# Where the modulation chunks and the next group's weights stand inside the down-projections of a SwiGLU

## The chip, the cores and the metric

The kernel runs on one core of a Trainium2 chip. The metric is the device time of one execution in microseconds (us). Before the change it was 2321.56 us, the median of three runs (2318.89, 2321.56 and 2325.57 us).

The engines are called PE (matrix products; PEld is its weight load), DVE (VectorE), ACT (ScalarE), POOL (GpSimd) and SP (SyncE, which here only issues DMA transfers).

## The reference

One inference step of a two-layer backbone, on 128 context rows and 512 latent rows of width 1024 (640 tokens in all). Each layer runs a SwiGLU, a mixer (layer 0: convolution and spatial gating; layer 1: windowed attention), and a second SwiGLU. Each of them is wrapped in a norm with a shift, a scale and a gate that come from the modulation vector:

```python
def modulation(cond, w_mod, b_mod):
    m = jax.nn.silu(cond) @ w_mod + b_mod
    return m.reshape(cond.shape[0], N_MOD, D_MODEL)       # 9 rows of 1024 per layer

def pre(x, m, g, slot):
    return rms_norm(x, g) * (1 + m[:, 3 * slot + 1][:, None, :]) + m[:, 3 * slot][:, None, :]

def residual(x, y, m, g, slot, weight):
    return x + weight * m[:, 3 * slot + 2][:, None, :] * rms_norm(y, g)

def swiglu(h, wg, wu, wd):                                # wg, wu: 1024 x 2816, wd: 2816 x 1024
    return (jax.nn.silu(h @ wg) * (h @ wu)) @ wd
```

All is float32. The modulation of both layers is read from `w_mod`, 2 x 1024 x 9216 numbers; the kernel reads it in 128-column chunks, of which 128 are worked in the background of the four SwiGLUs.

## The kernel before, in words

**Precision.** A float32 product is made of three products of halves: each weight chunk is loaded as a tile `raw` (128x1024 float32, 512 KB), ACT copies it into a rounded high half, DVE subtracts that from it for the low half (both tiles named `w`), and PE multiplies high by high, high by low and low by high.

**One SwiGLU.** `ffn` is called four times, layer by layer. The 2816 hidden columns are 22 tiles of 128, taken in parts: (0,5), (5,10), (10,16), (16,22) in the first SwiGLU, (0,4), (4,10), (10,16), (16,22) in the other three. A part computes its hidden tiles (gate, up, silu and product), and then `down` multiplies them with their rows of `wd`: ten steps (two halves of the output columns by five token tiles), each a run of PE products into one PSUM bank, an ACT copy `tmp<-ps` and a GpSimd transfer that adds it to `ys` in memory. The fourth part ends elsewhere (`last_products`).

**Groups.** The first tiles of a SwiGLU (ten in the first, four in the others) are computed the plain way. From tile `since` on `group` computes a tile by seven products p1 to p7 of sums, each of 12 matmuls with 320 columns. Their weights come from one array `ws` in three loads: G (512 KB, `load_gate`, into `raw`), the sums S (`load_sums`, into `rawx`, with an adding GpSimd transfer behind the load) and U (`load_up`, for two tiles at once, into `raw`). From them come these steps, named as in the code; a 0 is the ACT copy and a 1 the DVE subtraction:

- g0, g1: the halves of G (for p2, p1)
- s2: two DVE additions that turn G's buffer into weight sums; t0, t1: the halves of these (for p3, p6)
- s0, s1: the halves of S (for p7, p5)
- u0, u1: the halves of U (for p4)

A product is moved out of PSUM by e1 to e7: e1, e3, e5, e6 on ACT, e2, e4, e7 on DVE. p6 is accumulated in the bank of p1 and p5 in the same bank again, so p6 can start only behind e1 and p5 only behind e6. Inside a group the first tile's products come in the order p1, p2, p6, p7, p5. `go` runs a product, then the evacuation of the product before, then one entry of a list of fills, which prepare the next tile.

**The transition.** The weights of a group's first tile are prepared inside `down` of the part before: the list `between` has one entry for each of its ten steps, and the list `mods` says how many modulation chunks follow each step. In the text a step is called by its place: down step 0 to down step 9. The second tile's weights (written g0', g1' and so on) are prepared by the fills of the first tile's products, the third tile's are written g0'' and so on.

**Chunks.** `mod_chunk` takes one modulation chunk: a load of 512 KB from `wmodT` into `raw` by SP (line 536), then two DVE passes (`scr<-raw,cbc`, one for each of the two conditions), each with a short read of the accumulator. `background(n)` takes the next n chunks; `background_ahead` only issues the load of the next one. In a transition the chunks are here called m1, m2 and so on, in their order. Chunks are queued as 54, 33, 33 and 8 for the four SwiGLUs; the last one's list is used up within its first `down` and the group after it. Nine transitions into a group carry chunks: one behind a part of five tiles (first SwiGLU), five behind parts of six tiles (one in the first, two in the second, two in the third SwiGLU) and three behind parts of four tiles (second, third and fourth).

**What sets the order.** PE, DVE, ACT and POOL run in program order; nothing overtakes. SP issues its transfers in program order as well, and a transfer that waits for its buffer holds back all that stand behind it. The tile `raw` has three buffers in turn, so a load waits for the last reader of the third load before it. `rawx` has two. The loads of `wd`, of G, of U and of the chunks all share `raw`.

Of the kernel before, what the change touches and what calls it, by code (L numbers as in the profile page):

```python
# [89 lines left out]
class Builder:  # L90
# [548 lines left out]
    def ffn(self, l, i, h, lead, nxt, fetches, started=None):  # L639
# [9 lines left out]
        def weights(j):  # L649
            if j not in ws:  # L650
                ws[j] = [self.take(*self.ffn_weight(l, i, j, w)) for w in ("wg", "wu")]
            return ws[j]

        def unit(j, g, inserts=None):
            if j not in gs:
                gs[j] = self.pair()
            self.glu(*self.proj2(weights(j), h, g, inserts), gs[j], g)
# [24 lines left out]
        def load_sums(j):  # L682

            w = a["ws"][l, i, j]
            r = self.rawx()
            nc.sync.dma_start(out=r, in_=w[:, 512:1536])
            nc.gpsimd.dma_start(out=r.rearrange("p (a b) -> p a b", a=2),  # L687
                                in_=w[:, 1536:2048].unsqueeze(1).to_broadcast([P, 2, 512]), accum_op=ALU.add)
            raws["s", j] = r

        def load_gate(j):
            r = raws["g", j] = self.raw(D)
            nc.sync.dma_start(out=r, in_=a["ws"][l, i, j, :, 0:1024])

        def load_up(j):
            n = min(2, ends[j] - j)
            r = raws["u", j] = self.raw(n * 512)
            nc.sync.dma_start(out=r.rearrange("p (j m) -> p j m", j=n),
                              in_=a["ws"][l, i, j:j + n, :, 1024:1536].rearrange("j p m -> p j m"))
# [20 lines left out]
        def prep(j):  # L720


            def s2():
                r = raws["t", j] = raws["g", j]
                V.tensor_tensor(out=r[:, 512:1024], in0=raws["s", j][:, 512:1024], in1=r[:, 512:1024], op=ALU.add)
                V.tensor_tensor(out=r[:, 0:512], in0=r[:, 512:1024], in1=r[:, 0:512], op=ALU.add)

            g = halves("g", j, (2, j), (1, j))
            s = halves("s", j, (7, j), (5, j))
            t = halves("t", j, (3, j), (6, j))  # L730
            u = halves("u", j, (4, j), (4, j + 1)) if j in pairs else [lambda: None] * 2
            return dict(g0=g[0], g1=g[1], s2=s2, t0=t[0], t1=t[1], s0=s[0], s1=s[1], u0=u[0], u1=u[1])
# [68 lines left out]
        def run(fs):  # L801
            for f in fs:
                f()

        def wpieces(half, j0, j1):

            res = []

            def piece(j):
                m = min(2, j1 - j)  # L810
                res.extend(self.wload(a["wd"][l, i, j:j + m, :, half * 512:half * 512 + 512].rearrange("j p m -> p j m"), m, 512))

            return [lambda j=j: piece(j) for j in range(j0, j1, 2)], res
# [3 lines left out]
        def sums_between(every=1):  # L817
            return {k: lambda: run([tops.pop(0) for _ in range(1) if tops]) for k in range(0, KC, every)}
# [4 lines left out]
        def settle():  # L823

            for f, j in late[:]:
                if f is not p7 or (p5, j) in done:
                    late.remove((f, j))
                    evacs[f](j)
                    done.add((f, j))

        def go(f, j, *then):
            f(j)
            settle()
            late.append((f, j))
            run(then)

        def fills(n):

            if n >= NJ:
                return [[] for _ in range(7)]  # L840
            w = prep(n)
            return [[], [w["g0"]], [w["g1"]], [lambda: load_up(n), w["s2"]] if n in pairs else [w["s2"]], [w["t0"]],
                    [w["t1"], lambda: load_gate(n + 1) if n + 1 < ends[n] else None],
                    [w["s0"], w["s1"], lambda: load_sums(n + 2) if n + 2 < NJ else None]]

        def steps(j0, j1):

            r = [(p1, j0), (p2, j0), (p6, j0), (p7, j0), (p5, j0)]
            for j in range(j0 + 1, j1):
                r += [(p1, j), (p3, j - 1), (p6, j), (p4, j - 1), (p7, j), (p5, j), (p2, j)]  # L850
            return r

        def group(j0, j1, wd):


            fs = []
            ahead, mod = [self.background_ahead], [lambda: self.background(1)]
            for j in range(j0, j1):
                w = prep(j)
                f = fills(j + 1) if j + 1 < j1 else [[], [], wd[0:1], [], wd[1:2], [], wd[2:3]]  # L860
                u = [w["u0"], w["u1"]] if j in pairs else []
                if j == j0:
                    f = [u + ahead + f[1], f[2] + f[3], mod + f[4], f[5], ahead + f[6]]
                else:
                    f[0] = u + f[0]
                    if j + 1 < j1:
                        f[1] = f[1] + mod
                    if j + 2 < j1:
                        f[5] = f[5] + ahead
                fs += f  # L870
            for (p, j), f in zip(steps(j0, j1), fs):
                go(p, j, *f)
            go(p3, j1 - 1, *wd[3:4])
            go(p4, j1 - 1, *wd[4:])
            settle()
# [3 lines left out]
        def down(j0, j1, pi, wd):  # L879

            gp = [gs.pop(j) for j in range(j0, j1)]
            loads, wd2 = wpieces(1, j0, j1)
            if j1 < since:
                between = [loads, [], [], [], [], [], [lambda: weights(j1)], [], [], []]
                mods = [0, 2, 2, 1, 1, 1, 0, 1, 1, 1]
            else:
                n = prep(j1)
                between = [loads, [], [], [lambda: load_gate(j1)], [],
                           [n["g0"], n["g1"]], [n["s2"], n["t0"]], [n["t1"], lambda: load_gate(j1 + 1)],
                           [lambda: load_up(j1), n["s0"]], [n["s1"], lambda: load_sums(j1 + 2)]]  # L890
                mods = [0, 2, 2, 1, 1, 0, 0, 0, 0, 0]
            for half in range(2):
                for t in range(NT):
                    ps = self.ps()
                    self.proj_tok(ps, gp, (wd, wd2)[half], t)
                    o = self.tmp(512)
                    copy(o, ps)
                    nc.gpsimd.dma_start(out=ys[t, half], in_=o, **(dict(accum_op=ALU.add) if pi else {}))  # L898
                    run(between.pop(0))
                    self.background(mods.pop(0))  # L900

        for pi, (j0, j1) in enumerate(bounds[:-1]):
            loads, wd = wpieces(0, j0, j1)
            if j0 >= since:
                group(j0, j1, loads)
            elif not started:
                load_sums(since)
                load_sums(since + 1)
                unit(1, GB, sums_between())
                weights(3)  # L910
                unit(2, GB, sums_between())
                todo = sums_between()
                todo[2] = lambda then=todo[2]: (then(), run(loads))
                unit(3, GA, todo)
                run(tops)
                unit(3, GB)
            else:
                if j0 == 0:
                    unit(1, GB)
                    self.setup_cbc()  # L920
                    unit(2, GA)
                    weights(3)
                    self.background(2)
                    unit(2, GB)
                    self.background(2)
                else:
                    load_sums(since)
                    load_sums(since + 1)
                for j in range(max(j0, 3), j1):
                    weights(j)  # L930
                    if j + 1 < j1:
                        weights(j + 1)
                    else:
                        run(loads)
                    for n, g in enumerate(GROUPS):
                        unit(j, g, sums_between(2) if j0 else None)
                        self.background(1 if j0 else 2)
                if j0:
                    run(tops)
            down(j0, j1, pi, wd)  # L940
        j0, j1 = bounds[-1]
        rows = self.gate_rows(l, slot, True)
        wd = []
        group(j0, j1, [lambda j=j: wd.append(self.wload(a["wd"][l, i, j], 2, 512)) for j in range(j0, j1)])
        gp = [gs.pop(j) for j in range(j0, j1)]
        self.drain()
# [1014 lines left out]
```

## Time and profile before

| | us |
|---|---|
| median of three runs | 2321.56 |
| the profiled execution's own time | 2317.79 |
| its span in the trace | 2316.0 |
| PE busy | 2251.5 (97% of the span) |
| DVE busy | 1656.7 (72%) |
| ACT busy | 1048.5 (45%) |
| POOL busy | 282.2 (12%) |

The profiled execution took 1.8 us more than its span, and 3.8 us less than the median. A row of the trace's timeline reads: start, duration, engine, line, operation, output <- input, shape, count, and in brackets the idle time ahead of it with the instruction that ended it. Most rows carry line 71, the helper through which the engines' instructions are recorded, so rows are told apart by their tiles and shapes: `ps<-w,act` with 512 columns is the down-projection, `ps<-act,w` and `ps<-sum,w` with 320 columns are products of a group, `w<-raw,w` and `w<-rawx,w` on DVE are the steps whose names end in 1, and `scr<-raw,cbc` is a pass over a chunk.

### The profile page before, as it was taken

The numbers are of one execution on the slowest core, as the hardware profiler recorded it, in microseconds if no ns is written. First come the engines' busy times: TensorE is split into PE (matmuls) and PEld (weight loads), VectorE is DVE, ScalarE is ACT, GpSimd is POOL, SyncE is SP. The second block draws the span as 40 slices with busy tenths as digits, with TensorE's granted clock in tenths as the row PEclk, the third lists the DMA queues.
The fourth block names the chain that finished last, engine by engine and source line by source line (L and its number), as shares of the span: only waits on it lengthen the run. The fifth ranks groups of instructions, "written<-read, shape, count | busy, mean of one in ns | idle before, by whom it ended". The sixth has DMA issues, their size and how long they took to land.

```text
span 2316.0 us, 35260 instructions
## 1 busy us (share of the span) xinstructions
PE 2251.5 (97%) x13692; PEld 2039.6 (88%) x13692; DVE 1656.7 (72%) x2758; ACT 1048.5 (45%) x1845; POOL 282.2 (12%) x377
## 2 busy tenths in 40 slices
PE   9999999999999999999999999999989999999998
PEld 8989898989889898989798989898966798989896
DVE  5688777767867786868677777676788578636366
ACT  5223343453165443434554434345568564435352
POOL 1000111021002111110011011102121021111100
PEclk9999999999999999999999999999989999999999
DMA  8564868632224578785536687864000345666644
GB/s 306 169 231 153 220 180 213 187 139 89 76 101 124 183 196 200 192 199 162 217 111 209 181 213 179 212 189 154 36 21 10 128 120 192 171 135 156 140 125 173
DMA packets 137671, 370.07 MB, mean 160 GB/s; under 512 B 14464, under 2 KB 16384, under 8 KB 136736
## 3 DMA queue, kind: packets, MB, share of 16 engines
q1 hardware_dynamic: 103952, 299.93, 38.0%
q0 software_dynamic: 33552, 67.90, 16.8%
q8 instruction: 107, 1.75, 0.3%
q14 instruction: 60, 0.49, 0.1%
HBM read 322.90 MB, written 42.25 MB: 158 GB/s over the span
## 4 chain that ended last, share of the span: by engine, by line
PE 69%; DVE 14%; DMA 7%; issue 4%; ACT 4%; POOL 1%; SPq 1%; DVEq 0%; ACTq 0%; POOLq 0%
PE ps L71 69%; DVE tmp L71 4%; DVE w L71 2%; DVE scr L71 2%; DMA raw<-wmodT 2%; DMA ggrow<-grow 2%; ACT w L71 1%; DVE Y L71 1%; DMA Y<-ys 1%; DVE act L71 1%; POOL nwq L71 1%; ACT tmp L71 1%; DMA rawx<-ws 1%; ACT act L71 1%; DVE raw L71 1%
## 5 line engine op out<-in xcount | busy, mean ns | idle before, releaser
L71 PE MATMUL ps<-act,w 128*128 128x320 f32 (+6 forms) x6024 | 914.5, 319 | 18.5 <-DVE w L71 10.1
L71 PEld LDWEIGHTS ps<-act,w 128*128 128x128 f32 (+1 forms) x6024 | 847.6, 185 | 49.3 <-issue 18.1
L71 PE MATMUL ps<-w,act 128*128 128x512 f32 (+1 forms) x3480 | 793.0, 387 | 11.0 <-ACT act L71 7.8
L71 PEld LDWEIGHTS ps<-w,act 128*128 128x128 f32 x3480 | 632.1, 191 | 149.5 <-ACT act L71 9.7
L71 DVE TENSOR_TENSOR w<-raw,w 128x1024 fp32r<-128x1024 f32 (+1 forms) x340 | 410.7, 1221 | 191.2 <-ACT w L71 183.9
L71 PE MATMUL ps<-sum,w 128*128 128x320 f32 x3168 | 481.5, 310 | 6.9 <-ACT tmp L71 6.7
L71 PEld LDWEIGHTS ps<-sum,w 128*128 128x128 f32 x3168 | 469.1, 188 | 10.9 <-ACT tmp L71 10.9
L71 ACT ACTIVATE w<-raw 128x1024 fp32r<-128x1024 f32 (+1 forms) x340 | 350.7, 1047 | 163.2 <-DVE raw L71 76.9
L71 ACT ACTIVATE tmp<-ps 128x320 f32<-128x320 f32 (+4 forms) x450 | 210.1, 470 | 400.5 <-PE ps L71 314.5
L71 DVE CUSTOM_DVE_ANT_0 scr<-raw,cbc 128x1024 bf16<-128x1024 f32 x256 | 313.4, 1224 | 84.2 <-DMA raw<-wmodT 78.3
L71 ACT ACTIVATE act<-tmp 128x256 fp32r<-128x256 f32 (+4 forms) x238 | 114.9, 497 | 355.3 <-DVE tmp L71 355.2
L71 DVE TENSOR_TENSOR act<-tmp,act 128x256 fp32r<-128x256 f32 (+4 forms) x240 | 124.7, 528 | 116.5 <-ACT act L71 115.4
L898 POOL DMA_DIRECT2D ys<-tmp x120 | 91.2, 763 | 659.8 <-ACT tmp L71 646.3
L687 POOL DMA_DIRECT2D rawx<-ws x66 | 79.9, 1214 | 642.5 <-DMA rawx<-ws 234.9
L71 DVE TENSOR_TENSOR w<-rawx,w 128x1024 fp32r<-128x1024 f32 x66 | 80.8, 1224 | 39.7 <-ACT w L71 38.1
L71 DVE TENSOR_TENSOR tmp<-ps,tmp 128x320 f32<-128x320 f32 x132 | 63.9, 484 | 23.4 <-PE ps L71 22.6
L71 DVE TENSOR_TENSOR tmp<-tmp,tmp 128x640 f32<-128x640 f32 (+1 forms) x98 | 68.7, 715 | 6.4
L71 ACT ACTIVATE tmp<-ps,sh,G 128x256 f32<-128x256 f32 (+1 forms) x120 | 60.3, 525 | 22.2 <-PE ps L71 22.1
L71 ACT ACTIVATE w<-rawx 128x1024 fp32r<-128x1024 f32 x66 | 69.4, 1051 | 0.0
L71 ACT ACTIVATE Y<-X 128x1024 f32<-128x1024 f32 x30 | 31.7, 1058 | 80.9 <-DVE X L71 76.9
L71 DVE TENSOR_TENSOR tmp<-tmp,ps 128x320 f32<-128x320 f32 (+2 forms) x110 | 52.7, 479 | 18.0 <-ACT tmp L71 17.2
L71 PE MATMUL ps<-ident,Y 128*128 128x128 f32 x260 | 49.7, 286 | 15.1 <-DVE Y L71 14.4
(165 smaller groups left out, 1265.0 us busy)
## 6 DMA issues: line engine op xcount, KB each, us to landing
raw<-wmodT SPq DMA_DIRECT2D x128, 512.0 KB, 4.6
raw<-ws SPq DMA_DIRECT2D x99, 512.0 KB, 4.7
raw<-wd SPq DMA_DIRECT2D x86, 512.0 KB, 4.1
rawx<-ws SPq DMA_DIRECT2D x66, 512.0 KB, 4.9
rawx<-ws POOLq DMA_DIRECT2D x66, 512.0 KB, 6.9
ys<-tmp POOLq DMA_DIRECT2D x120, 256.0 KB, 4.7
raw<-wg SPq DMA_DIRECT2D x22, 512.0 KB, 4.7
raw<-wu SPq DMA_DIRECT2D x22, 512.0 KB, 3.5
```

Source lines behind the costliest of these rows:

```text
L71: i = method(*args, **kw)
L687: nc.gpsimd.dma_start(out=r.rearrange("p (a b) -> p a b", a=2), in_=w[:, 1536:2048].unsqueeze(1).to_broadcast([P, 2, 512]), accum_op=ALU.add)
L898: nc.gpsimd.dma_start(out=ys[t, half], in_=o, **(dict(accum_op=ALU.add) if pi else {}))
```

## The change

Four places in `ffn`, `group` and `down`:

```diff
 # group(), the fills of a group's first tile
-                    f = [u + ahead + f[1], f[2] + f[3], mod + f[4], f[5], ahead + f[6]]
+                    f = [u + f[1], f[2] + f[3], ahead + f[4], f[5], f[6] + mod + ahead]
 # down(), where no group follows (the first SwiGLU's first part)
-                between = [loads, [], [], [], [], [], [lambda: weights(j1)], [], [], []]
-                mods = [0, 2, 2, 1, 1, 1, 0, 1, 1, 1]
+                between = [loads, [], [], [], [], [lambda: weights(j1)], [], [], [], []]
+                mods = [0, 2, 2, 1, 0, 0, 1, 1, 1, 1]
 # down(), where a group follows
-                           [n["g0"], n["g1"]], [n["s2"], n["t0"]], [n["t1"], lambda: load_gate(j1 + 1)],
-                           [lambda: load_up(j1), n["s0"]], [n["s1"], lambda: load_sums(j1 + 2)]]
-                mods = [0, 2, 2, 1, 1, 0, 0, 0, 0, 0]
+                           [n["g0"], n["g1"]], [n["s2"], n["t0"]], [n["t1"], self.background_ahead],
+                           [lambda: load_gate(j1 + 1), n["s0"], n["s1"]], [lambda: load_up(j1), lambda: load_sums(j1 + 2)]]
+                mods = [0, 1, 1, 1, 1, 0, 0, 0, 1, 1]
 # ffn(), the first SwiGLU's start, behind the third tile's second half
-                    self.background(2)
+                    self.background(3)
```

A transition carries six chunks inside `down` in both versions: before, at steps 1 (two), 2 (two), 3 and 4; now at steps 1, 2, 3, 4, 8 and 9. The load of m5 is issued at step 7, behind t1. In the first SwiGLU's first `down` there are nine chunks in place of ten, with the plain tile's weights (`weights(j1)`) one step sooner, and the tenth is taken ahead of it. The number of chunks in all, the arithmetic and the bytes moved stay as they are.

The order of the instructions shows it at the transition of the second SwiGLU from tiles 4–9 to the group of tiles 10–15. DVE before; `w<-rawx,w` is s1, the first `w<-raw,w` u1 (from `raw_1567`), the second g1' (from `raw_1564`), the two with 512 columns s2', `tmp<-tmp,ps` e2, and the last row the first pass of m7:

```order
L71 TENSOR_TENSOR w_1569_9029<-rawx_1479_8476,w_1568_9028 128x1024
L71 TENSOR_TENSOR w_1575_9071<-raw_1567_9026,w_1574_9070 128x1024
L71 TENSOR_TENSOR w_1578_9077<-raw_1564_9002,w_1577_9076 128x1024
L71 TENSOR_TENSOR raw_1564_9002<-rawx_1497_8603,raw_1564_9002 128x512
L71 TENSOR_TENSOR raw_1564_9002<-raw_1564_9002 128x512
L71 TENSOR_TENSOR tmp_1580_9092<-tmp_1580_9092,ps_1579_9079 128x320
L71 ISA scr_1582_9111,mraw1_105<-raw_1576_9074,cbc_813 128x1024
```

DVE at the same place of the changed kernel; the passes over m5 read `raw_1558`, those over m6 `raw_1570` (each first pass is shown; its accumulator read and the second pass are left out):

```order
L71 TENSOR_TENSOR w_1563_9017<-rawx_1479_8476,w_1562_9016 128x1024
L71 ISA scr_1564_9020,mraw1_105<-raw_1558_8990,cbc_813 128x1024
...
L71 ISA scr_1571_9053,mraw1_105<-raw_1570_9051,cbc_813 128x1024
...
L71 TENSOR_TENSOR w_1575_9071<-raw_1568_9046,w_1574_9070 128x1024
L71 TENSOR_TENSOR w_1577_9075<-raw_1561_9014,w_1576_9074 128x1024
L71 TENSOR_TENSOR raw_1561_9014<-rawx_1497_8603,raw_1561_9014 128x512
```

Between s1 and u1 there stood nothing, and now there stand four passes. In the older order the passes over m5 and m6 stand ahead of g1.

SP's transfers at the same place before; `raw_1546` and `raw_1551` are m5 and m6, `raw_1564` is G of the second tile, `raw_1567` U, `raw_1576` m7, `raw_1588` G of the third tile:

```order
L536 DMA raw_1546_8892<-wmodT 128x1024
L536 DMA raw_1551_8920<-wmodT 128x1024
L693 DMA raw_1564_9002<-ws 128x1024
L698 DMA raw_1567_9026<-ws 128x2x512
L536 DMA raw_1576_9074<-wmodT 128x1024
L686 DMA rawx_1572_9054<-ws 128x1024
L693 DMA raw_1588_9137<-ws 128x1024
```

and in the changed kernel, where `raw_1558`, `raw_1570` and `raw_1581` are m5, m6 and m7, and `raw_1561`, `raw_1568` and `raw_1585` are G of the second tile, U and G of the third:

```order
L536 DMA raw_1558_8990<-wmodT 128x1024
L693 DMA raw_1561_9014<-ws 128x1024
L698 DMA raw_1568_9046<-ws 128x2x512
L686 DMA rawx_1569_9048<-ws 128x1024
L536 DMA raw_1570_9051<-wmodT 128x1024
L536 DMA raw_1581_9109<-wmodT 128x1024
L693 DMA raw_1585_9129<-ws 128x1024
```

The load of m6 moved from ahead of G and U to behind the next sums, and it is the third load of `raw` behind m5: with three buffers it is given m5's own, so it waits for m5's second pass. The same stands at all nine transitions with chunks.

## The prediction, made before the changed kernel ran

> **What bounds the kernel now.** The page comes first.
>
> ```profile
> span 2316.0 us, 35260 instructions
> PE 2251.5 (97%) x13692; PEld 2039.6 (88%) x13692; DVE 1656.7 (72%) x2758; ACT 1048.5 (45%) x1845; POOL 282.2 (12%) x377
> raw<-wmodT SPq DMA_DIRECT2D x128, 512.0 KB, 4.6
> ```
>
> PE is the bound: it is idle for 64 us in all. An edit that touches no product can gain only from those 64 us, and loses wherever PE waits for something new. So the second view is that of PE's waits, of which the change can reach this group:
>
> ```profile
> PE ps L71 <- ACT tmp L71: 13.1, 15, 2.5
> ```
>
> These are the waits for evacuations at the starts of groups: 13.1 us in 15 waits. The third view is the timeline of one transition, that of the order rows above (a part of six tiles, P = 914.02 being the start of p1).
>
> ```profile
> 872.23 41.95 PE L71 MATMUL ps<-w,act 128*128 128x512 f32 x180
> ...
> 887.78 1.22 DVE L71 CUSTOM_DVE_ANT_0 scr<-raw,cbc 128x1024 bf16<-128x1024 f32 x1
> ...
> 890.31 1.23 DVE L71 CUSTOM_DVE_ANT_0 scr<-raw,cbc 128x1024 bf16<-128x1024 f32 x1
> ...
> 910.09 0.60 ACT L71 ACTIVATE tmp<-ps 128x512 f32<-128x512 f32 x1 [1.79 <-issue]
> 910.58 1.05 ACT L71 ACTIVATE w<-rawx 128x1024 fp32r<-128x1024 f32 x1
> 911.66 1.23 DVE L71 TENSOR_TENSOR w<-rawx,w 128x1024 fp32r<-128x1024 f32 x1 [2.60 <-ACT w L71]
> 914.02 3.65 PE L71 MATMUL ps<-act,w 128*128 128x320 f32 x24
> 914.76 2.00 ACT L71 ACTIVATE w<-raw 128x1024 fp32r<-128x1024 f32 x2
> 915.85 2.36 DVE L71 TENSOR_TENSOR w<-raw,w 128x1024 fp32r<-128x1024 f32 x2 [2.96 <-ACT w L71]
> 917.51 5.66 PE L71 MATMUL ps<-sum,w 128*128 128x320 f32 x36
> 918.24 0.69 DVE L71 TENSOR_TENSOR raw<-rawx,raw 128x512 f32<-128x512 f32 x1
> 918.97 0.69 DVE L71 TENSOR_TENSOR raw<-raw 128x512 f32<-128x512 f32 x1
> 919.70 1.06 ACT L71 ACTIVATE w<-raw 128x1024 fp32r<-128x1024 f32 x1 [2.61 <-DVE raw L71]
> 920.66 0.41 ACT L71 ACTIVATE tmp<-ps 128x320 f32<-128x320 f32 x1
> ```
>
> Read from the bottom. The last row is e6, ended at 921.07. PE's 36 matmuls from 917.51 are p6, p7 and p5, so p5 starts after two thirds of 5.66 us, at about 921.2: e6 is done as p5 begins, with no slack. In front of e6 on ACT stands t0' (919.70), which waited 2.61 us for s2' on DVE (918.24 and 918.97); s2' stands behind u1 and g1' (915.85). This chain takes 921.07 - 915.85 = 5.22 us from the start of u1. Whatever delays u1 delays p5 by as much. In front of u1 DVE is idle for 2.96 us, behind s1 (911.66, ended 912.89): this is the room the change fills.
>
> **The change, part by part: the transitions.** One chunk takes DVE 2.53 us (890.31 - 887.78). At down steps 8 and 9 the change puts m5 and m6 between s1 and u1.
>
> m5 costs nothing here. Its load is issued behind t1 and has the time of three steps (4.2 us each, 41.95/10) to land; its passes fill 912.89 to 915.42, and u1 waited until 915.85 anyway.
>
> m6 is different, since its load can't be issued before m5's second pass gives its buffer back. What a load of this kind takes from issue to use, three times:
>
> ```profile
> 805.21 0.33 SPq L536 DMA_DIRECT2D raw<-wmodT  x1
> ...
> 812.00 1.23 DVE L71 CUSTOM_DVE_ANT_0 scr<-raw,cbc 128x1024 bf16<-128x1024 f32 x1 [4.14 <-DMA raw<-wmodT]
> ...
> 922.50 0.33 SPq L536 DMA_DIRECT2D raw<-wmodT  x1
> ...
> 926.88 1.23 DVE L71 CUSTOM_DVE_ANT_0 scr<-raw,cbc 128x1024 bf16<-128x1024 f32 x1 [1.32 <-DMA raw<-wmodT]
> ...
> 936.31 0.33 SPq L536 DMA_DIRECT2D raw<-wmodT  x1
> ...
> 939.71 1.22 DVE L71 CUSTOM_DVE_ANT_0 scr<-raw,cbc 128x1024 bf16<-128x1024 f32 x1 [0.23 <-DMA raw<-wmodT]
> ```
>
> 6.8, 4.4 and 3.4 us; the page's median over all 128 is 4.6, which I take, and 3.4 and 6.8 are the ends. So u1 starts 2.53 + 4.6 + 2.53 = 9.66 us behind the end of s1, and p5 starts 9.66 + 5.22 = 14.88 us behind it. In the part of six tiles that is 912.89 + 14.88 = 927.8 in place of 921.1: 6.7 us later, with nothing for PE to do meanwhile, since p1, p2, p6 and p7 are done by P + 7.3 and all that follows stands behind p5. Five times, 33.5 us.
>
> The Trainium skill ("DMA: Bandwidth & Descriptors", section on the anatomy of one DMA) has a fit of 2.0 us + bytes/436e3, stated for GpSimd's path; for these 524288 bytes it gives 3.2 us, an estimate by that page, under the shortest of the three rows. By it the sum would be about 13 us smaller; the median of 128 loads decides.
>
> In the other transitions s1's end follows from P: it comes behind the copy of step 8 (910.09 = P - 4.2 + 0.26), by 912.89 - 910.09 = 2.80. So s1 ends at P + 3.07 minus one step, and a step lasts as its tiles: 4.2, 3.5 or 2.8 us for six, five or four. That gives P - 1.1, P - 0.4 and P + 0.3. In before, these four transitions stand as follows (the first row of each begins at P; the row that gives p5's start comes last, and for the third p5 is the last third of the 36):
>
> ```profile
> 258.99 3.67 PE L71 MATMUL ps<-act,w 128*128 128x320 f32 x24
> ...
> 268.41 2.03 PE L71 MATMUL ps<-sum,w 128*128 128x320 f32 x12 [0.21 <-ACT tmp L71]
> ...
> 794.89 3.65 PE L71 MATMUL ps<-act,w 128*128 128x320 f32 x24
> ...
> 803.85 2.03 PE L71 MATMUL ps<-sum,w 128*128 128x320 f32 x12 [0.20 <-ACT tmp L71]
> ...
> 1243.15 3.66 PE L71 MATMUL ps<-act,w 128*128 128x320 f32 x24
> 1249.31 7.10 PE L71 MATMUL ps<-sum,w 128*128 128x320 f32 x36 [2.50 <-ACT tmp L71]
> 1256.25 3.66 PE L71 MATMUL ps<-act,w 128*128 128x320 f32 x24
> ...
> 1955.59 3.68 PE L71 MATMUL ps<-act,w 128*128 128x320 f32 x24
> ...
> 1962.98 2.03 PE L71 MATMUL ps<-sum,w 128*128 128x320 f32 x12 [0.18 <-ACT tmp L71]
> ```
>
> p5 now starts at P - 0.4 + 14.88 = 273.4 (before 268.4: +5.0), and at P + 0.3 + 14.88 = 810.1 (803.85: +6.2), 1258.3 (before about 1256.25 - 1.9 = 1254.4: +3.9) and 1970.8 (1962.98: +7.8). Sum 22.9. The gain that the change brings is in here: with m5 and m6 out of the way, g1, s2, t1 and s1 keep pace with ACT, and the short waits at these starts go. All nine together: 33.5 + 22.9 = 56.4.
>
> **The change: the clock behind a stall.** Two stretches of the windows view, with the granted clock behind PE's idle time (1.76 us of it ended at 264.42, 2.50 us at 1249.31):
>
> ```profile
> 1250.00:1253.00 3.00, 3.00 (x14) 3.00 (x13) 2.93 (x5) 1.14 (x2) 0.00 (x0) 0.50 1.02 366
> 260.00:265.00 5.00, 3.23 (x23) 2.97 (x22) 4.10 (x4) 4.37 (x7) 2.61 (x3) 1.00 0.55 124
> ```
>
> Behind 2.50 us the clock was 0.50 and the 36 matmuls took 7.10 us, where the same 36 took 5.66 at 917.51: 1.4 us lost. Behind the shorter one it stayed at 1.00. The new stalls are 13.75 - 7.3 = 6.5 us or more, so I charge each with 1.5: 9 x 1.5 = 13.5 (bounds: nothing, and 3 us each if the half clock holds twice as long). The Trainium skill ("TensorE: Matmul & The Clock Gate", Part 1) halves the clock after an idle window of some 3.4 us; by it, too, every one of these stalls would be charged. The trace goes further, with a drop behind 2.50 us.
>
> A PE that comes 1.5 us later finds the evacuations of the group's later tiles further on. Of the 13.1 us about half lies there; I give back 3.6.
>
> m7 now stands ahead of e7, and its load behind t1' (m6's delay included: issued at 928.7, landed 933.3, passed 935.8). e7 ends at 936.3; p4 comes four products (7.3 us) behind p5, at 935.1, or 936.6 with the slow clock. I charge nothing; with a load of 6.8 us it would be 2 us each. G'' stands behind that load on SP, issued at 929.1 and landed at 933.7; its ACT copy ends by 934.8 and the e6 behind it is wanted by p5 of the second tile, three products behind that p4: covered.
>
> **The change: the first SwiGLU's start.** The same 22 chunks are taken ahead of its first group, one of them sooner.
>
> ```profile
> 109.00:145.00 36.00, 32.51 (x139) 25.87 (x139) 30.85 (x49) 7.86 (x12) 3.84 (x7) 0.99 0.71 253
> 144.66 1.01 PE L71 MATMUL ps<-act,w 128*128 128x384 f32 x2 [3.49 <-ACT w L71]
> ```
>
> DVE is busy for 30.85 of 36 us there and is what PE waits for. The chunk taken sooner adds up to 2.5 us ahead of the down-projection; the wait of 3.49 us at 144.66 loses about as much, since the weights come a step sooner. As DVE has the same work up to the next tile, I take -0.5, with 2.5 to both sides.
>
> **The sum.** 56.4 + 13.5 - 3.6 - 0.5 = 65.8 on the profiled execution's 2317.8, so 2383.6. The median of the runs lies 3.8 above that execution, so 2387.
>
> **The rivals.**
>
> *Faster: the waits at the group starts go, and m6 finds its place in idle time.* The 13.1 us and some of the 3.49 are what there is to gain; DVE is idle for 28% of the span, and g1 to s1 are freed from m5 and m6. Time: 2321.6 - 13 = about 2309. It decides where m6 delays u1 by under a microsecond, so m6 would need a buffer ahead of time; against it stand the order rows, by which it has m5's. Chance 0.06.
>
> *m6's load is hidden after all, and only its passes count.* Then u1 comes 2.53 us behind 915.42, at 917.95, 2.1 us late: 10.5 for the five, and 4.6 less than above for the others (0.4 + 1.6 + 0 + 3.2), 15.7 in all. Stalls of about 2 us lie at the edge where the clock falls; at none, 2337. Chance 0.08.
>
> *No change.* The chunks are as many as before, and DVE has room. It needs every transition to come out within 0.8 us (7 us over nine), m6's load and passes hidden, and the waits of before to stay. Chance 0.05.
>
> *The stall as forecast, but no clock lost or a short load:* 2387 - 13.5 = 2373 without the clock's part; with loads of 3.4 us another 11 less, 2363. With loads of 6.8 us 9 x 2.2 = 20 more, 2407. These are my forecast's own bounds; it has 0.81 with them.
>
> **How the numbers follow.** Two executions of this kernel differ by up to 7 us (2318.89 to 2325.57), so 0.3%, 7 us, is about what can be told from no change. Faster 0.06; same 0.06, the case above and a little of the second rival; slower 0.88. The forecast's bounds are 2363 to 2407, and 2412 with a little of m7's 2 us; to leave out no more than 2 in 10 the lower end goes down to 2352, where part of m6's load is hidden.
>
> **What would show it.** In the new trace, at each of the nine transitions: DVE idle 4 to 5 us between the passes of m5 and m6, ended by the chunk's load; u1 some 6.7 us later than now against P; a PE wait of 6 to 8 us for ACT `tmp` ahead of 12 matmuls `ps<-sum,w`, so this group of waits near 60 us; PEclk 0.50 behind it. PE's waits for 2 us in place of 6.5 would show the load hidden; no waits at all and a shorter group start the first rival. I am wrong if u1 stands at P + 2 as before, or if the time is lost elsewhere.

## The result, and the profile after

The changed kernel takes 2401.11 us (median of four runs, 2399.78 to 2402.85), the kernel before beside it 2322.81 us (2318.89 to 2325.57): the recorded ratio is 1.0349, 95% interval 1.0333 to 1.0365 (the two medians give 1.0337). That is 78 us slower, where 2387 (66 us on the profiled execution) was forecast with a range of 2352 to 2412.

The page of the changed kernel, with the group of PE's products on the sums:

```profile
span 2400.5 us, 35251 instructions
PE 2264.2 (94%) x13692; PEld 2053.3 (86%) x13692; DVE 1656.5 (69%) x2758; ACT 1056.7 (44%) x1845; POOL 282.6 (12%) x377
...
L71 PE MATMUL ps<-sum,w 128*128 128x320 f32 x3168 | 493.7, 314 | 78.2 <-ACT tmp L71 78.2
```

PE has the same 13692 matmuls and is busy 12.7 us longer (2251.5 before); the windows view below shows the lower clock that goes with it. DVE is busy as long as before; the loss is not work. The wait of PE's products for ACT is the other part. PE's waits, of the changed kernel:

```profile
PE ps L71 <- ACT tmp L71: 80.9, 14, 9.6
PE ps L71 <- DVE w L71: 15.4, 13, 6.6
```

The first row was 13.1 us: 67.8 us more. With the 12.7 us of longer matmuls that is 80.5 of the 84.5 us between the two profiled executions' spans; the rest is changes of other waits. That for DVE `w` (second row) was 10.4 us; it grew at the first SwiGLU's start, where a wait for ACT `w` shrank. The nine long ones, from the timeline of PE, eight here and one, at 953, in the next view:

```profile
275.03 3.57 PE L71 MATMUL ps<-sum,w 128*128 128x320 f32 x12 [7.10 <-ACT tmp L71]
...
401.09 3.57 PE L71 MATMUL ps<-sum,w 128*128 128x320 f32 x12 [8.74 <-ACT tmp L71]
...
826.34 3.57 PE L71 MATMUL ps<-sum,w 128*128 128x320 f32 x12 [7.18 <-ACT tmp L71]
...
1080.24 3.57 PE L71 MATMUL ps<-sum,w 128*128 128x320 f32 x12 [9.10 <-ACT tmp L71]
...
1303.46 3.57 PE L71 MATMUL ps<-sum,w 128*128 128x320 f32 x12 [6.29 <-ACT tmp L71]
...
1431.58 3.57 PE L71 MATMUL ps<-sum,w 128*128 128x320 f32 x12 [9.47 <-ACT tmp L71]
...
1558.86 3.41 PE L71 MATMUL ps<-sum,w 128*128 128x320 f32 x12 [9.58 <-ACT tmp L71]
...
2044.62 3.57 PE L71 MATMUL ps<-sum,w 128*128 128x320 f32 x12 [8.95 <-ACT tmp L71]
```

All are p5 of a group's first tile, 12 matmuls that took 1.9 to 2.0 us before and now take 3.4 to 3.6. The four behind parts of five and four tiles (275, 826, 1303, 2044) waited 29.5 us, the five behind parts of six tiles 45.7. One of these, the transition that the prediction worked through (P is 937.23 now), with the engines in order of time; a row that ends in `x2` holds two instructions, the SP row here the issues of m6's and of m7's load:

```profile
934.87 1.23 DVE L71 TENSOR_TENSOR w<-rawx,w 128x1024 fp32r<-128x1024 f32 x1 [6.50 <-ACT w L71]
936.01 1.22 DVE L71 CUSTOM_DVE_ANT_0 scr<-raw,cbc 128x1024 bf16<-128x1024 f32 x1
936.12 0.33 SPq L686 DMA_DIRECT2D rawx<-ws  x1
...
938.54 9.85 SPq L536 DMA_DIRECT2D raw<-wmodT  x2
...
942.26 1.21 POOL L687 DMA_DIRECT2D rawx<-ws  x1 [3.04 <-DMA rawx<-ws]
945.53 1.23 DVE L71 CUSTOM_DVE_ANT_0 scr<-raw,cbc 128x1024 bf16<-128x1024 f32 x1 [7.02 <-DMA raw<-wmodT]
...
947.95 2.35 DVE L71 TENSOR_TENSOR w<-raw,w 128x1024 fp32r<-128x1024 f32 x2
...
951.06 0.69 DVE L71 TENSOR_TENSOR raw<-raw 128x512 f32<-128x512 f32 x1
...
951.79 1.06 ACT L71 ACTIVATE w<-raw 128x1024 fp32r<-128x1024 f32 x1 [11.50 <-DVE raw L71]
952.75 0.42 ACT L71 ACTIVATE tmp<-ps 128x320 f32<-128x320 f32 x1
...
953.22 3.57 PE L71 MATMUL ps<-sum,w 128*128 128x320 f32 x12 [8.82 <-ACT tmp L71]
```

s1 ends at 936.1, m5's passes follow at once, m6's load is issued at 938.54 as m5's second pass ends, and DVE stands idle for 7.02 us for it. u1 starts at 947.95, 10.7 us behind P where it was 1.8 before; s2', t0' and e6 follow, and p5. The clock behind it, from the windows view:

```profile
953.30:956.50 3.20, 3.20 (x12) 3.20 (x13) 3.15 (x4) 0.81 (x1) 0.00 (x0) 0.50 0.39 132
```

The clock is 0.50 or 0.51 behind the other eight as well. In the windows that follow this one it is 0.50 up to 957.0, 0.61 up to 958.0 and 1.00 up to 959.0, so the half clock lasts for some 4 us, past p5's matmuls.

The theory to be tested: m6's load, issued only when m5 gives its buffer back and standing in front of u1, stalls p5, and the clock falls behind the stall. Rivals: the DVE passes in front of u1 cost by themselves; the later loads, the new fills or the first SwiGLU's start do it.

### The profile page after: what moved, and what is told of

It is laid out like the page before. It is cut to its first block, busy times and chain, and to the rows that moved or that the text cites. A ratio compares the mean times of both kernels' runs of the same rounds, so it can differ in the third digit from the quotient of the medians.

```text
span 2400.5 us, 35251 instructions
## 1 busy us (share of the span) xinstructions
PE 2264.2 (94%) x13692; PEld 2053.3 (86%) x13692; DVE 1656.5 (69%) x2758; ACT 1056.7 (44%) x1845; POOL 282.6 (12%) x377
## 3 DMA queue, kind: packets, MB, share of 16 engines
q0 software_dynamic: 33552, 67.90, 16.2%
## 4 chain that ended last, share of the span: by engine, by line
PE 74%; DVE 12%; DMA 6%; issue 3%; ACT 2%; POOL 1%; SPq 0%; DVEq 0%; ACTq 0%; POOLq 0%
PE ps L71 74%; DVE tmp L71 3%; DVE w L71 3%; DMA raw<-wmodT 3%; DVE scr L71 2%; DMA ggrow<-grow 2%; DVE Y L71 1%; DMA Y<-ys 1%; ACT w L71 1%; ACT tmp L71 1%; DVE raw L71 1%; DVE act L71 1%; ACT act L71 0%; POOL nwq L71 0%; DVE nwq L71 0%
## 5 line engine op out<-in xcount | busy, mean ns | idle before, releaser
L71 PE MATMUL ps<-sum,w 128*128 128x320 f32 x3168 | 493.7, 314 | 78.2 <-ACT tmp L71 78.2
L71 PEld LDWEIGHTS ps<-sum,w 128*128 128x128 f32 x3168 | 480.3, 193 | 81.7 <-ACT tmp L71 81.7
L71 PE MATMUL ps<-ident,Y 128*128 128x128 f32 x260 | 48.3, 281 | 13.5 <-DVE Y L71 13.2
```

The costliest lines, as they stand in the source:

```text
L71: i = method(*args, **kw)
```

## The experiments

**One chunk behind s1.** The changed kernel with

```diff
-                mods = [0, 1, 1, 1, 1, 0, 0, 0, 1, 1]
+                mods = [0, 2, 1, 1, 1, 0, 0, 0, 1, 0]
```

> The changed kernel with one chunk instead of two behind s1: down takes its six chunks as 2, 1, 1, 1 at steps 1 to 4 and one at step 8, whose load is issued at step 7; everything else of the change stays. Theory (the second chunk behind s1 is loaded only when the first has given its buffer back, and u1 stands behind it): the stalls ahead of p5 are gone, and the time falls to 2322 or a little less, 2312 to 2322, since g1 to s1 are no longer behind m5 and m6. Rival (DVE passes in front of u1 cost what they last, loads play no part): half of the loss stays, about 2360. Rival (the loads' new places or the new fills of the group do it): about 2400, as the changed kernel.

2321.84 us, ratio to the kernel before 1.0006 (0.9994 to 1.0019). The whole loss is gone once the second chunk stands elsewhere, so neither the passes of one chunk behind s1 nor the rest of the change carries it. The gain that was also expected isn't there: this kernel's waits of PE for ACT are

```profile
PE ps L71 <- ACT tmp L71: 14.2, 9, 3.6
```

as many as before (13.1), now at p6 behind parts of five and four tiles (3.1, 3.6, 1.3 and 2.1 us).

**m6's load left out.** The changed kernel, in which the passes over m6 read m5's tile again:

```diff
+        def again():
+            if self.bg:
+                self.modraws[self.bg[0][0]] = self.lastraw
-                           [lambda: load_gate(j1 + 1), n["s0"], n["s1"]], [lambda: load_up(j1), lambda: load_sums(j1 + 2)]]
+                           [lambda: load_gate(j1 + 1), n["s0"], n["s1"]], [lambda: load_up(j1), lambda: load_sums(j1 + 2), again]]
```

(with `self.lastraw` set in `mod_chunk`).

> The changed kernel with m6's load left out: the passes over m6 read m5's tile again, so the modulation is wrong and 512 KB less is read at each of the nine transitions. DVE's instructions and their order are as in the changed kernel. Theory (the serial load is most of the loss): u1 at s1's end + 5.1 us, 2.1 us late at the five transitions of six tiles and 0 to 3 at the others, clock kept: 2322 + 10 to 16, about 2335. Rival (DVE's passes in front of u1 are the loss, whenever their data comes): at most 9 x 1 us better than the changed kernel, about 2390.

2336.42 us, ratio 1.0067 (1.0049 to 1.0086). Of the 78 us 65 go with the load. What is left is 17 us over the kernel before measured beside this run (2319.63). The passes of m6 still stand in front of u1, and PE's waits ahead of p5 are 0.6 to 3.2 us at the nine transitions. The same transition in this kernel's timeline (P is 917.21):

```profile
919.79 1.22 DVE L71 CUSTOM_DVE_ANT_0 scr<-raw,cbc 128x1024 bf16<-128x1024 f32 x1
...
920.95 2.35 DVE L71 TENSOR_TENSOR w<-raw,w 128x1024 fp32r<-128x1024 f32 x2
...
926.22 2.03 PE L71 MATMUL ps<-sum,w 128*128 128x320 f32 x12 [1.84 <-ACT tmp L71]
```

u1 follows m6's second pass, 1.9 us later than before against P (3.74 instead of 1.83), PE waits 1.84 us, and p5 runs at full clock. At the transitions of four tiles the wait is 3.0 to 3.2 us, and there the clock falls (0.50 and 0.56 at the first two; p5 takes 2.96 us at the third). It also falls at one transition of six tiles, behind 2.27 us (0.53; p5 takes 3.39 us). This is the rival of the prediction that was priced at 2337.

**The next sums behind m6's load.** The changed kernel with `load_sums(j1 + 2)` taken out of `down` and put into the group's first fill:

```diff
-                    f = [u + f[1], f[2] + f[3], ahead + f[4], f[5], f[6] + mod + ahead]
+                    f = [u + f[1] + [lambda: load_sums(j0 + 2)], f[2] + f[3], ahead + f[4], f[5], f[6] + mod + ahead]
```

> The changed kernel with the load of the next sums (load_sums) issued behind the load of m6, in the first fill of the group, instead of ahead of it. In the changed kernel m6's load took 7.0 us from issue to use where the sums' load and its adding transfer ran beside it, 4.7 to 5.8 elsewhere. Theory (traffic beside it makes m6's load long): the load falls to about 4.6 us, 2.4 us less at the five transitions of six tiles and up to 1 us at the other four: 2401 - 14 = 2387. Rival (a load of this kind takes what it takes): 2401. If the sums themselves then come late, slower than 2401.

2400.99 us, ratio 1.0342 (1.0321 to 1.0364). It tells nothing: in the built program SP still has the sums' load ahead of m6's (issued at P - 1.1, m6's at P + 1.3). Unlike what the part on the kernel before says, SP's order is not that of the code: the kernel holds only the instructions of PE, DVE, ACT and POOL to it, and the transfers that SP and GpSimd issue stand where the build puts them. Here it put the sums' load, which was ready, ahead of m6's, which had to wait. So the order was tied, and the sums put further back:

```diff
+                    f = [u + f[1], f[2] + f[3], ahead + f[4], [lambda: load_sums(j0 + 2, True)] + f[5], f[6] + mod + ahead]
...
+            if behind and self.bg:
+                self.tc.add_manual_dep(ld.ins, self.modld.ins.name, mybir.DependencyInfo(
+                    mybir.DependencyClass.NoSync, mybir.DependencyReason.DATA), reason="order")
```

> What the run before it (sums later) was to show and didn't, since the build put the sums' load ahead of m6's on SP all the same: the changed kernel with the load of the next sums tied behind the loads of m6 and m7 on SP, so that m6's load runs with no sums' load or adding transfer beside it. Theory (traffic beside it makes m6's load long): m6's load takes 4 to 5 us at the five transitions of six tiles instead of 7.0, and the time falls by 5 x 2.5 and some us of the others, 2401 to about 2386. Rival (the load's length is its own, or comes from the ys transfers, which stay): 2401.

2381.17 us, ratio 1.0268 (1.0247 to 1.0288), 20 us less than the changed kernel. Its timeline at the same transition (P is 932.50; the first row again holds m6's and m7's loads):

```profile
933.81 6.84 SPq L536 DMA_DIRECT2D raw<-wmodT  x2
...
937.79 1.23 DVE L71 CUSTOM_DVE_ANT_0 scr<-raw,cbc 128x1024 bf16<-128x1024 f32 x1 [4.01 <-DMA raw<-wmodT]
...
940.74 0.38 SPq L686 DMA_DIRECT2D rawx<-ws  x1
...
945.49 3.50 PE L71 MATMUL ps<-sum,w 128*128 128x320 f32 x12 [5.82 <-ACT tmp L71]
```

Without the sums beside it the load takes 4.0 us from issue to use, where it took 7.0 with them; DVE waits 4.01 instead of 7.02 us, and PE 5.82 instead of 8.82. Over the nine transitions m6's loads take 3.6 to 4.5 us in place of 4.7 to 7.7, 36 us in all in place of 57, and the time falls by 20. So the part of m6's load that goes here is traffic, shown for the 3 us of this transition and the 21 of all nine; the 4 us that stay aren't parted further.

**The clock.** 36 matmuls on h, into a PSUM bank that nobody reads, between p7 and p5 of the first tile:

```diff
+                if chunks and p is p5 and j == j0:
+                    warm()
                 go(p, j, *f)
```

> The changed kernel with 36 matmuls of 320 columns on the input h, into a PSUM bank that nobody reads, between p7 and p5 of a group's first tile at the nine transitions with chunks: about 5.7 us of work inside stalls of 6.3 to 9.6 us. Theory (a part of the loss is the granted clock, halved behind a stall; p5's 12 matmuls took 3.57 us there instead of 2.03 or less): the stall's end stays where it is, p5 and the products behind it run at full clock, 1.6 to 2.8 us less at each of nine: 2401 - 15 to 25, about 2381. Rival (the clock plays no part; p5 is slow for another reason, such as its operands): 2401.

2392.29 us, ratio 1.0308 (1.0283 to 1.0333): 9 us less than the changed kernel, under what was expected. At eight of the nine transitions PE was still idle for 2.3 to 4.1 us before p5 (0.9 us at the ninth, where m6's load happened to take 4.3 us), and p5 took 2.0 to 3.4 us. Hence more of them:

```diff
+                    warm(18 if before == 6 else 14)
```

> As the run with 36 idle-time matmuls, but with 54 of them (about 8.5 us) in the transitions of six tiles and 42 (6.6 us) in the others, so that PE has hardly any idle time before p5: the first such run left 2.3 to 4.1 us idle, and its p5 took 2.0 to 3.4 us instead of 3.57. Theory (the halved clock behind the stall costs 1.6 us or more at each of nine): p5's 12 matmuls in 2.1 us or less at all nine, and 2401 - 15 to 20, about 2383, if m6's loads last as long as in the changed kernel. Rival (the clock's part is what the first run gained): 2392.

2383.54 us, ratio 1.0272 (1.0252 to 1.0292), 17.6 us less than the changed kernel, with 438 matmuls more. From its page, and p5 of two of its transitions:

```profile
PE 2312.4 (97%) x14130; PEld 2102.1 (88%) x14130; DVE 1656.9 (70%) x2758; ACT 1053.9 (44%) x1845; POOL 283.1 (12%) x377
```

```profile
276.92 3.37 PE L71 MATMUL ps<-sum,w 128*128 128x320 f32 x12 [2.98 <-ACT tmp L71]
...
952.62 2.03 PE L71 MATMUL ps<-sum,w 128*128 128x320 f32 x12 [1.07 <-ACT tmp L71]
```

p5 still comes at P + 16.2 in the second, against P + 16.0 in the changed kernel, and takes 2.03 us, as at seven of the other eight (2.03 or 2.05). At the first, with 2.98 us left idle, the clock fell all the same (0.51). Over the nine the stalls end 1.1 us sooner in sum than in the changed kernel, since m6's loads were a little shorter; the rest, some 16 us or nearly 2 us a transition, is the clock's part, with some 6 us to either side by the intervals of the two ratios.

**The other parts of the change.** First the group's new fills alone, on the kernel before:

```diff
-                    f = [u + ahead + f[1], f[2] + f[3], mod + f[4], f[5], ahead + f[6]]
+                    f = [u + f[1], f[2] + f[3], ahead + f[4], f[5], f[6] + mod + ahead]
```

> The kernel before with the change's new fills of a group's first tile alone: m7's load issued two products later, m7's passes behind s1' instead of ahead of t1', m8's load as before behind them. Theory: t1', s1' and e7 come 2.5 us sooner and nothing waits for m7, so no difference that can be told: 2320 within 4 us, perhaps a little less at the second tile's waits. Rival (m8's load comes later and g1'' waits behind m8's passes): 2324 to 2330.

2320.10 us, ratio 0.9993 (0.9982 to 1.0004). Then the first SwiGLU's start alone (its `between` and `mods`, and three chunks behind the third tile):

```diff
-                mods = [0, 2, 2, 1, 1, 1, 0, 1, 1, 1]
+                mods = [0, 2, 2, 1, 0, 0, 1, 1, 1, 1]
```

> The kernel before with the change's edits of the first SwiGLU's start alone (three chunks behind the third tile, weights(j1) at step 5, nine chunks in its down). Theory: no difference that can be told, 2322 within 3 us; in the changed kernel the first group's down starts 0.5 us later than before. Rival (the extra chunk ahead or the sooner weights matter): 2 to 5 us to one side.

2320.75 us, ratio 1.0007 (0.9996 to 1.0019). Neither makes a difference that can be told. Last, the changed kernel with the chunks at their old steps, its loads and fills kept:

```diff
-                mods = [0, 1, 1, 1, 1, 0, 0, 0, 1, 1]
+                mods = [0, 2, 2, 1, 1, 0, 0, 0, 0, 0]
```

> The changed kernel with the six chunks at their old steps (2, 2, 1, 1 at steps 1 to 4), all else of the change kept: G and U of the group's first two tiles a step later, s1 at step 8, m7's load at step 7, the group's new fills, the first SwiGLU's start. Theory (the chunks behind s1 are the whole loss): 2322 within 5 us, with the waits of before at the transitions of four and five tiles. Rival (the later loads and the new fills carry part of the loss): 2330 to 2400.

2333.79 us, ratio 1.0065 (1.005 to 1.008): not nothing, against the theory. The transition from the part of five tiles, in this kernel's timeline (P is 260.36):

```profile
261.16 1.22 DVE L71 TENSOR_TENSOR w<-raw,w 128x1024 fp32r<-128x1024 f32 x1 [1.13 <-ACT w L71]
...
262.41 0.38 SPq L698 DMA_DIRECT2D raw<-ws  x1
...
268.02 2.00 ACT L71 ACTIVATE w<-raw 128x1024 fp32r<-128x1024 f32 x2 [4.48 <-DMA raw<-ws]
```

U's load is issued at 262.41, as t1 (261.16) gives G's buffer back, 2.05 us behind P; in the kernel before it was issued 2.9 us ahead of P. The load issued at step 7 is m7's here, whose passes come only behind s1': it holds one of the three buffers, so U waits for another. ACT waits for U ahead of e1, and p6 stalls 6.4, 5.4, 3.4 and 4.3 us at the four transitions of five and four tiles, none at those of six. So a load issued ahead holds a buffer until its passes have run, and here the later weights paid for it. The kernel with one chunk behind s1 issues the same load ahead and takes its passes before u1; its p6 waits less at all four.

**Five chunks.** Two versions with five chunks in `down`, the sixth in the group's last tile. On the changed kernel:

```diff
-                mods = [0, 1, 1, 1, 1, 0, 0, 0, 1, 1]
+                mods = [0, 1, 1, 1, 1, 0, 0, 0, 1, 0]
-                    if j + 1 < j1:
-                        f[1] = f[1] + mod
-                    if j + 2 < j1:
+                    f[1] = f[1] + mod
+                    if j + 1 < j1:
```

> The changed kernel with five chunks in down instead of six, at steps 1, 2, 3, 4 and 8, and the sixth taken in the group's last tile, which had none; loads and fills else as in the changed kernel. Theory (a chunk behind s1 is free as long as its load was issued ahead; two in a row aren't): no stalls of 6 to 10 us, and at the transitions of four and five tiles fewer chunks stand ahead of g1, so s1 ends by P + 0.3 and of the 10 us that stood there before (1.8, 1.3, 2.5 us and later ones) some 5 to 8 go: 2312 to 2320. Rival (any chunk behind s1 delays u1 and p5): slower than before, 2330 or more. Rival (the kernel before had nothing left there): 2322.

2313.24 us, ratio 0.9974 (0.9963 to 0.9984). And on the kernel before, with `mods = [0, 2, 1, 1, 1, 0, 0, 0, 0, 0]` and the same lines of `group`:

> The kernel before with five chunks in down instead of six (2, 1, 1, 1 at steps 1 to 4) and the sixth in the group's last tile, nothing else of the change. It parts the two things that the five-chunk version of the changed kernel did. Theory (what is gained is that fewer chunks stand ahead of g1 at the transitions of four and five tiles): part of the 6 us, about 2316. Rival (the gain is the fifth chunk's place behind s1 and the new places of the loads): 2320, as the kernel before.

2314.33 us, ratio 0.9975 (0.9965 to 0.9984). Both beat the kernel before by 6 us, and by the same. PE's waits for ACT, of the first and of the second version:

```profile
PE ps L71 <- ACT tmp L71: 5.7, 7, 1.6
```

```profile
PE ps L71 <- ACT tmp L71: 7.5, 12, 1.6
```

Of the 13.1 us 7.4 and 5.6 go, about as many as the time falls. What the two share is one chunk less ahead of the group, so that is the likely gain, wherever the fifth stands; a place behind s1 gains nothing more that these runs can tell.

## Why the prediction was right, and where its sizes were off

- **m6 in front of u1.** Right as worked out: u1 waits for m5's passes, m6's load and m6's passes, and p5 for e6 behind it (in the transition shown u1 starts at P + 10.7 and p5 at P + 16.0, 5.3 us later; forecast 5.22). The signs named ahead of time are there: DVE idle for m6's load at all nine (4.7 to 7.9 us; 4 to 5 was forecast), PE's waits behind it (6.3 to 9.6; forecast 6 to 8) and PEclk 0.50. The loss is undone by moving one chunk in `mods`, and 65 us of it by leaving out the load alone.
- **Its price at parts of five and four tiles.** p5 was put at P + 14.4, 15.2, 15.2 and 15.2 and came at P + 15.5, 15.1, 15.2 and 16.2: 25.0 us later than before in sum, where 22.9 was forecast.
- **Its price at parts of six tiles** is the term that was too small: 6.5 us of idle time each was forecast and 8.7 to 9.6, 9.1 in the mean, was measured, 13 us over the five. m6's load was taken at 4.6 us, the median over the whole kernel; in front of it on SP the next sums' load had just been issued, with an adding transfer behind, and it took 6.9 to 7.7 us at the five, above even the 6.8 that the prediction took as its upper end. That traffic stood in the order rows of the changed kernel, and a row with 6.8 us stood among those quoted. These 13 us are most of what the forecast lacks, by the medians (78 against 66) and by the two profiled executions, on which the sum was made (84.5 against 65.8).
- **The clock.** 13.5 us forecast; PE is busy 12.7 longer, and filling the stalls won 17.6, of which some 16 is the clock. The window of before in which the clock was read as kept behind 1.76 us (260 to 265) holds only 0.6 us behind that wait; the stretch 264.5 to 268.2 shows 1.00 too, so the reading stands. The Trainium skill ("TensorE: Matmul & The Clock Gate", Part 1) halves the clock after an idle window of some 3.4 us, and the trace agrees behind stalls of 6 to 10 us (0.50); the drops behind 2.27 and 2.98 us of idle time are earlier than that.
- **The waits given back.** 3.6 us; the later waits of before, 4.2 us at 286, 288, 821, 823, 1283, 1980 and 1982, have no successor in the changed kernel. Right.
- **m7 and G''.** The step was wrong without a price. m7's load was put behind t1'; it was issued at P + 10.8, as m6's second pass ended, and G'' at P + 12.0, as u1 ended. By these times the three buffers of `raw` did not go round in turn, as was assumed, but each to the next load in the order of their release. For m6 both rules name m5's buffer, so the main step was not touched.
- **The first SwiGLU's start.** -0.5 with 2.5 to both sides; alone it is 1.0007 (0.9996 to 1.0019). In the changed kernel the wait of 3.49 us is 0.46 us, waits for DVE `w` ahead of the second part's down-projection have grown about as much, and that down-projection starts 0.5 us later. No difference that can be told, within its bounds.
- **Rivals.** "Faster" would have needed m6's load ahead of time; even with one chunk behind s1 the 13 us of waits did not go. The rival with the load hidden was priced at 2337 and is the run without the load, 2336; that they meet so closely is in part luck, since the clock fell at four of its nine transitions and the rival charged nothing for it.

What stays open: which traffic the 3 us are due to, the sums' load or its adding transfer, since both were moved together; what makes up the 4 us that a load takes without it; and 4 of the 84.5 us between the two profiled executions.

## What to carry to other kernels

Before work is moved into an idle slot, ask of each piece whether its data can be there when the slot begins: count the buffers that are held at that place, and find whose release the load waits for. The first piece moved here was free, with its load issued ahead; the second turned 2.5 us of work into a stall of 6 to 10 us. For the price of such a load, take what else is in flight at that place, not the median of the kernel; and count what a stall costs behind its end as well, here nearly 2 us of half clock on PE each time.

## What the runs showed of the hardware

- In the changed kernel m6's load of 512 KB took 4.7 to 7.7 us from issue to use, with the sums' load issued 2.4 to 2.5 us ahead of it and an adding transfer issued before it was used; with these two put behind it, it took 3.6 to 4.5 us. The Trainium skill's fit ("DMA: Bandwidth & Descriptors", anatomy of one DMA), stated for GpSimd's path, gives an estimate of 3.2 us; no load of m6 was that short.
- PE's granted clock was 0.51 behind 2.98 us of idle time (stalls filled), 0.53 behind 2.27 us (m6's load left out) and 0.50 behind 2.50 us (the kernel before). It stayed at 1.00 behind 1.07 and 1.87 us (stalls filled) and behind 2.34 us (36 filling matmuls). With one chunk behind s1 it fell behind 2.07 us, some 1 us after PE had started again (1.00, then 0.81, then 0.50). So these runs give no single idle time at which it falls.
- In the changed kernel the half clock lasted through p5's 12 matmuls, 3.57 us for 2.03.
